# Where the activation combinations of the up-projection's first pass are computed: GpSimd or VectorE

## The chip, the core and the metric

The kernel runs on one core of a Trainium2 chip. A core has five engines that each work through a queue of their own, in order: TensorE (PE in the profile; its weight loads are PEld), VectorE (DVE), ScalarE (ACT), GpSimd (POOL) and SyncE (SP), which here only issues transfers. The engines wait for each other through semaphores. Transfers run on DMA queues; SP issues nearly all of them, in order, and a transfer that has to wait holds those behind it. The metric is the time of one execution on the device in microseconds, as a median of several runs.

## The reference

One layer of a hybrid decoder block on 2048 tokens of width 1024, all in float32: an RMSNorm, an input projection into two head groups (a gated DeltaNet and a retention group), an output projection with a residual, then the part that matters here:

```python
n2 = _rms_norm(h, mlp_norm_w[l])
h = h + _conv_glu_mlp(n2, w_up[l], mlp_conv_w[l], w_down[l])

def _conv_glu_mlp(x, w_up, conv_w, w_down):
    hdn = jnp.einsum('bsd,df->bsf', x, w_up)
    hdn = _causal_dwconv(hdn, conv_w)
    g, u = jnp.split(hdn, 2, axis=-1)
    return jnp.einsum('bsf,fd->bsd', jax.nn.silu(g) * u, w_down)
```

The up-projection has 2 × 2816 columns, the convolution is causal, depthwise, of width 3. A final RMSNorm follows.

## The kernel before

The program has three stages: the mixers, with the output projection and the second norm (about the first 1200 us), the up-projection (to about 1850 us), and the down-projection. Tokens go in four blocks of 512.

**Products.** Two ideas shape the matrix products. First, each float32 operand is split into a high half (a copy in a shorter format, made by ScalarE) and a low half (the original less the high one, made by VectorE); a product is three matmuls, high by high (line 118), high by low (119) and low by high (120). Where TensorE waits for a low half, the row shows VectorE as the releaser. Second, the products are done on 2 × 2 blocks with seven products in place of eight. For that both sides need sums and differences of blocks. `comb` makes them: in `prep_x` for the activations (line 1121), in `load_w` for the weights (line 1151). Their split is in `split` (ScalarE line 1101, VectorE line 1102).

**The up-projection.** It runs in two passes q over the tokens, each of 1024 tokens (two blocks), and in each pass over 22 groups g of columns. `prep_x(q)` loads the normed activations of the pass from DRAM (`xr`, line 1113), in four k-tiles of four blocks b11, b12, b21, b22; each tile gives four combinations, two of them chained:

```python
t1 = comb(5, ALU.subtract, b12, b11)
t2 = comb(6, ALU.subtract, b22, t1)
t3 = comb(7, ALU.subtract, b22, b12)
t4 = comb(4, ALU.subtract, b21, t2)
```

and then seven operands are split, b11, b21, b22 and the four combinations. So a pass has 16 combinations of 128 × 512 and 28 splits. They stay in SBUF for the whole pass. `xr` has seven buffers, and `st`, which holds combinations of activations and of weights, has four. The weights of a group come as two loads (`wur`, line 1144). The products of a group are in `group`; its sums on VectorE are line 1183, and the convolution is line 1225.

**The handover.** The last block's output projection is still under way when the up-projection's first pass starts: its operands are split in lines 1045 and 1046, its results are added to `Cw` in line 1017 (which frees the accumulator in PSUM), with `x` from `wx` (line 1022), and stored to `hd` (1027). A fence holds back the first loads of the pass until certain transfers of the output projection have been issued. From about 1173 to 1223 us of the span all this is mixed: output projection, `prep_x(0)`, the weights of the first groups, the first products.

**What sets the order.** Every engine's queue is put together at build time by a list scheduler of the framework, which goes by its own estimate of each instruction's duration on its engine. So an instruction that is given to another engine also changes the order of its neighbours, on all engines. The second pass's `prep_x(1)` (about 1616 to 1652 us) runs the same lines.

Of the kernel before, what the change touches and what calls it, by code (L numbers as in the profile page):

```python
# [73 lines left out]
def unit(pool, tag, shape, dt=F32, **kw):  # L74

    n = int(np.prod(shape[1:]))
    t = pool.tile([P, U1], dt, tag=tag, name=tag, **kw)[:, :n]
    if len(shape) == 3:
        t = t.rearrange("p (a b) -> p a b", a=shape[1])
    elif len(shape) == 4:  # L80
        t = t.rearrange("p (a b c) -> p a b c", a=shape[1], b=shape[2])
    return t
# [1009 lines left out]
def mlp_up(ctx, tc, marks, drp, mm3, mcw, mhalo, n2d, wud, aud, w_u):  # L1092
    nc = tc.nc
    PE, ACT, DVE, POOL = nc.tensor, nc.scalar, nc.vector, nc.gpsimd
# [5 lines left out]
    def split(dst, src, lo_eng=DVE):  # L1100
        ACT.activation(dst[:, 0], src, AF.Copy)
        lo_eng.tensor_tensor(dst[:, 1], src, dst[:, 0].bitcast(F32), op=ALU.subtract)  # L1102

    def prep_x(q, fence=None):
        xc = {}
        for kt in range(4):
            qs = []
            for i in range(2):
                xr = unit(up, "xr", [P, 2, TB], bufs=NXR)
                k = 4 * i + kt  # L1110
                for t in range(2):
                    with tc.issue_after(fence[kt]) if fence else nullcontext():
                        nc.sync.dma_start(xr[:, t], n2d[2 * q + t, k // 2][k % 2])
                qs += [xr[:, 0], xr[:, 1]]
            b11, b12, b21, b22 = qs

            sts = [unit(up, "st", [P, 2, TB], bufs=NST) for j in range(2)]

            def comb(i, op, a, b_):
                t = sts[i // 6][:, (i - 4) % 2]  # L1120
                (POOL if q == 0 else DVE).tensor_tensor(t, a, b_, op=op)  # L1121
                return t
            t1 = comb(5, ALU.subtract, b12, b11)
            t2 = comb(6, ALU.subtract, b22, t1)
            t3 = comb(7, ALU.subtract, b22, b12)
            t4 = comb(4, ALU.subtract, b21, t2)
            for i, src in ((1, b11), (2, b21), (5, t1), (6, t2), (7, t3), (4, t4), (3, b22)):
                x_ = xc[i, kt] = unit(xp, f"x{i}_{kt}", [P, 2, TB], F32R, bufs=1)
                split(x_, src)
        return xc  # L1130
# [340 lines left out]
```

## Time and profile before

| | |
|---|---|
| median of 3 runs | 2479.42 us (2477.21 to 2479.72) |
| the profiled execution | 2480.82 us, its span 2479.0 us |
| TensorE busy | 2415.2 us (97%) |
| VectorE busy | 1653.4 us (67%) |
| ScalarE busy | 1008.5 us (41%) |
| GpSimd busy | 570.4 us (23%) |
| mean granted TensorE clock | 0.992 |

A row of a group tells the line, the engine and the operation, the written and the read tiles, and a count. Rows of a timeline give start and length in us; a row with "x3" is three instructions in a row, and its length goes from the first's start to the last's end. VectorE's records overlap a little: an instruction of 0.68 us is followed by the next start after 0.60 us, so starts are what is to be compared. Behind `<-` in brackets stands how long the engine had stood idle, and what ended it. "busy" of TensorE says that a matmul was in flight, not that it ran at its best pace; the count per time tells that.

### The profile page before, as it was taken

What the parts mean: (1) busy time and instruction counts of PE and PEld (TensorE: products, weight loads), DVE (VectorE), ACT (ScalarE), POOL (GpSimd) and SP (SyncE); (2) the same over time, 40 slices, a digit from 0 to 9 for tenths busy, and PEclk for the clock granted to TensorE, in tenths of its full rate; (3) what the DMA queues carried; (4) which work ended last, traced back from release to release, by engine and by line L of the source; (5) the groups of instructions that cost most, each with busy time, mean ns of one, the idle gap of its engine ahead of it and who ended that gap; (6) DMA issues with size and microseconds to landing.
All of it is one profiled execution on the core that took longest, in us unless ns stands there. A gap on an engine that the chain in (4) does not pass through costs nothing. (4 is left out here: it accounts for less than half of the span.)

```text
span 2479.0 us, 35810 instructions
## 1 busy us (share of the span) xinstructions
PE 2415.2 (97%) x12508; PEld 2024.7 (82%) x12508; DVE 1653.4 (67%) x3244; ACT 1008.5 (41%) x2125; POOL 570.4 (23%) x881
## 2 busy tenths in 40 slices
PE   9989899999999999998899999999999999999998
PEld 7877788888878888787688888878888888888887
DVE  5876865454654646436989889896575567555783
ACT  5655634344522544234554343442232224333341
POOL 1385214700183114521400110100000001422030
PEclk9999999999999999999899999999999999999999
DMA  5887866674565565647587788776646869764782
GB/s 214 292 293 276 310 223 233 238 254 163 199 227 192 188 242 177 220 149 257 192 323 289 290 307 299 293 296 251 228 147 242 282 241 292 260 209 144 234 258 97
DMA packets 281572, 590.05 MB, mean 238 GB/s; under 512 B 40560, under 2 KB 120880, under 8 KB 281392
## 3 DMA queue, kind: packets, MB, share of 16 engines
q1 hardware_dynamic: 264528, 573.40, 65.6%
q10 hardware_dynamic: 16864, 14.37, 1.9%
q8 instruction: 98, 1.61, 0.3%
q14 instruction: 82, 0.67, 0.1%
HBM read 395.42 MB, written 192.25 MB: 237 GB/s over the span
## 5 line engine op out<-in xcount | busy, mean ns | idle before, releaser
L119 PE MATMUL p<-x,wu 128*128 128x512 f32 x1176 | 460.5, 392 | 6.3 <-DVE x L1102 6.3
L118 PE MATMUL p<-x,wu 128*128 128x512 f32 x1176 | 455.4, 392 | 2.4 <-DVE Cw L1017 1.8
L120 PE MATMUL p<-x,wu 128*128 128x512 f32 x1176 | 452.9, 391 | 0.9 <-DVE wu L1102 0.9
L561 PE MATMUL tok<-wc,n 128*128 128x512 f32 (+2 forms) x768 | 275.7, 362 | 6.0 <-ACT n L449 5.7
L562 PE MATMUL tok<-wc,n 128*128 128x512 f32 (+2 forms) x768 | 274.8, 359 | 0.0
L563 PE MATMUL tok<-wc,n 128*128 128x512 f32 (+2 forms) x768 | 273.8, 360 | 0.0
L119 PEld LDWEIGHTS p<-x,wu 128*128 128x128 f32 x1176 | 221.9, 189 | 55.2 <-DVE x L1102 9.7
L118 PEld LDWEIGHTS p<-x,wu 128*128 128x128 f32 x1176 | 222.2, 189 | 52.6 <-DVE uc L1183 2.7
L120 PEld LDWEIGHTS p<-x,wu 128*128 128x128 f32 x1176 | 221.9, 189 | 47.2 <-DVE wu L1102 1.4
L1225 DVE SCALAR_TENSOR_TENSOR acc<-uc,base,acc 128x1023 f32<-128x1023 f32 (+1 forms) x176 | 221.1, 1279 | 41.8 <-ACT acc L1222 41.6
L1183 DVE TENSOR_TENSOR uc<-p,uc 128x512 f32<-128x512 f32 x224 | 153.0, 686 | 109.5 <-PE p L120 109.0
L118 PE MATMUL d<-v,uu 128*128 128x512 f32 x448 | 174.3, 389 | 0.0
L119 PE MATMUL d<-v,uu 128*128 128x512 f32 x448 | 174.3, 389 | 0.0
L120 PE MATMUL d<-v,uu 128*128 128x512 f32 x448 | 174.3, 389 | 0.0
L220 POOL TENSOR_TENSOR vt<-vr 128x512 f32<-128x512 f32 x33 | 51.2, 1561 | 514.9 <-DVE u L1307 421.2
L561 PEld LDWEIGHTS tok<-wc,n 128*128 128x128 f32 x768 | 145.4, 190 | 25.6 <-ACT n L449 5.7
L563 PEld LDWEIGHTS tok<-wc,n 128*128 128x128 f32 x768 | 145.3, 189 | 19.9
L562 PEld LDWEIGHTS tok<-wc,n 128*128 128x128 f32 x768 | 145.4, 189 | 19.2
L119 PE MATMUL chm<-n,wc 128*128 128x512 f32 x384 | 151.7, 395 | 0.0
L118 PE MATMUL chm<-n,wc 128*128 128x512 f32 x384 | 151.6, 395 | 0.0
L120 PE MATMUL chm<-n,wc 128*128 128x512 f32 x384 | 151.6, 395 | 0.0
L771 POOL TENSOR_TENSOR pers<-Nb,pers 128x248 f32<-128x248 f32 (+30 forms) x248 | 120.1, 484 | 71.8 <-DMA Nb<-z 55.9
(258 smaller groups left out, 4843.4 us busy)
## 6 DMA issues: line engine op xcount, KB each, us to landing
wu<-wu SPq DMA_DIRECT2D x280, 512.0 KB, 6.4
wc<-wd SPq DMA_DIRECT2D x166, 512.0 KB, 5.4
wv<-wo SPq DMA_DIRECT2D x112, 512.0 KB, 6.2
wd<-wc SPq DMA_DIRECT2D x60, 512.0 KB, 4.5
ur<-au SPq DMA_DIRECT2D x56, 512.0 KB, 5.3
wur<-in_w_u SPq DMA_DIRECT2D x48, 512.0 KB, 5.6
au<-st SPq DMA_DIRECT2D x88, 256.0 KB, 4.3
vr<-in_w_d SPq DMA_DIRECT2D x77, 256.0 KB, 5.1
```

Of the source, the lines that this page charges most:

```text
L118: PE.matmul(ps, ah, bh, start=(first and i == 0), stop=False, skip_group_check=chk)
L119: PE.matmul(ps, ah, bl, start=False, stop=False, skip_group_check=chk)
L120: PE.matmul(ps, al, bh, start=False, stop=(i == n - 1), skip_group_check=chk)
L220: POOL.tensor_tensor(tt[:, j], a, b_, op=ALU.subtract)
L561: PE.matmul(ps, ah, wh, start=(k == 0), stop=False)
L562: PE.matmul(ps, ah, wl, start=False, stop=False)
L563: PE.matmul(ps, al_, wh, start=False, stop=(k == KT - 1))
L771: POOL.tensor_tensor(tm[:, :, :n], Nb[:, j:j + 1, j + 1:].to_broadcast([P, 8, n]), X[:, :, j:j + 1].to_broadcast([P, 8, n]), op=ALU.mult)
L1183: add = lambda o, ps, a: DVE.tensor_tensor(o, ps, a, op=ALU.add)
L1225: DVE.scalar_tensor_tensor(acc[:, t:], u[:, :T2 - t], w, acc[:, t:], op0=ALU.mult, op1=ALU.add)
```

## The change

In `prep_x` the engine of the combinations was GpSimd in the first pass and VectorE in the second; now it is VectorE in both. Formulas, order in the source, fences, buffers and the loads are as they were.

```diff
             def comb(i, op, a, b_):
                 t = sts[i // 6][:, (i - 4) % 2]
-                (POOL if q == 0 else DVE).tensor_tensor(t, a, b_, op=op)
+                DVE.tensor_tensor(t, a, b_, op=op)
                 return t
```

Since the scheduler puts the queues together anew, neighbours move as well. The first place is VectorE's queue at the start of the handover. `st` written from `xr` (line 1121) is a combination of activations, `st` from `wur` one of weights; `wu` with a number is an operand of the output projection, `wu` without one a weight of the first group.

```order
 L1151 TENSOR_TENSOR st<-st,wur 128x512
+L1121 TENSOR_TENSOR st<-xr 128x512
 L1017 TENSOR_TENSOR Cw<-wo,Cw 128x512
 L1151 TENSOR_TENSOR st<-wur,st 128x512
 L1046 TENSOR_TENSOR wu_12009<-co,wu_12009 128x512
-L1102 TENSOR_TENSOR wu<-st,wu 128x512 x3
+L1102 TENSOR_TENSOR wu<-st,wu 128x512 x2
+L1121 TENSOR_TENSOR st<-xr,st 128x512
+L1121 TENSOR_TENSOR st<-xr 128x512
+L1102 TENSOR_TENSOR wu<-st,wu 128x512
```

The combinations of the first k-tile now stand between the splits of the first group's weights, and the rest are spread over the next 50 places.

The second place is VectorE's queue at the end of the handover, up to the split of the last combination of the last k-tile, `x_3_12254`; the number behind `x_` is the k-tile. Before:

```order
L1102 TENSOR_TENSOR x_3_12245<-st,x_3_12245 128x512
L1151 TENSOR_TENSOR st<-wur 128x512
L1102 TENSOR_TENSOR x_3_12257<-xr,x_3_12257 128x512
L1017 TENSOR_TENSOR Cw<-wo,Cw 128x512
L1102 TENSOR_TENSOR x_2_12221<-st,x_2_12221 128x512
L1151 TENSOR_TENSOR st<-st,wur 128x512
L1102 TENSOR_TENSOR x_3_12248<-st,x_3_12248 128x512
L1151 TENSOR_TENSOR st<-wur 128x512
L1102 TENSOR_TENSOR x_3_12251<-st,x_3_12251 128x512
L1151 TENSOR_TENSOR st<-wur,st 128x512
L1102 TENSOR_TENSOR x_3_12254<-st,x_3_12254 128x512
```

And the same end in the changed kernel:

```order
L1102 TENSOR_TENSOR x_3_12245<-st,x_3_12245 128x512
L1017 TENSOR_TENSOR Cw<-wo,Cw 128x512
L1151 TENSOR_TENSOR st<-wur 128x512
L1102 TENSOR_TENSOR x_2_12221<-st,x_2_12221 128x512
L1017 TENSOR_TENSOR Cw<-Cw,wx 128x512
L1121 TENSOR_TENSOR st<-xr,st 128x512
L1102 TENSOR_TENSOR x_3_12251<-st,x_3_12251 128x512
L1102 TENSOR_TENSOR x_3_12248<-st,x_3_12248 128x512
L1151 TENSOR_TENSOR st<-st,wur 128x512
L1151 TENSOR_TENSOR st<-wur 128x512
L1017 TENSOR_TENSOR Cw<-wo,Cw 128x512
L1102 TENSOR_TENSOR x_3_12254<-st,x_3_12254 128x512
```

Two additions of the output projection have moved in front of the last split, and the last weight combination behind it.

The third place is SP's queue, where the loads of the next group's weights stand between loads of activations (`xr`; those numbered 71 to 74 are already for the second pass), loads of `x` (`wx`) and stores of the output projection's result (`hd`). Before:

```order
L1113 DMA xr<-n2d_1_72 128x512
L1144 DMA wur<-in_w_u 128x1024
L1022 DMA wx<-in_x 128x512
L1144 DMA wur<-in_w_u 128x1024
L1027 DMA hd_82<-Cw 128x1024
L1022 DMA wx<-in_x 128x512
```

Now:

```order
L1022 DMA wx<-in_x 128x512
L1113 DMA xr<-n2d_1_72 128x512
L1022 DMA wx<-in_x 128x512
L1027 DMA hd_82<-Cw 128x1024
L1144 DMA wur<-in_w_u 128x1024 x2
```

Both loads of the weights now stand behind the last load of `x` and one more store.

## The prediction

> **What bounds the kernel now.** I read the page first (busy shares, the 40 slices), then the waits of TensorE from the up-projection on, and then the place that the change touches, in windows and instruction by instruction.
>
> ```profile
> span 2479.0 us, 35810 instructions
> PE 2415.2 (97%) x12508; PEld 2024.7 (82%) x12508; DVE 1653.4 (67%) x3244; ACT 1008.5 (41%) x2125; POOL 570.4 (23%) x881
> ```
>
> TensorE is the bound of the whole. So GpSimd's share is worth nothing by itself; a change to it pays only where TensorE stands still. The windows show such a place (columns: stretch, its length, busy time and count of each engine, the granted TensorE clock, DMA share, GB/s):
>
> ```profile
> core 0: us, PE busy (x) PEld busy (x) DVE busy (x) ACT busy (x) POOL busy (x), PEclk, DMA share, GB/s
> 1173.30:1222.70 49.40, 35.95 (x114) 24.82 (x113) 49.40 (x55) 21.95 (x39) 30.12 (x17) 0.83 0.58 202
> 1222.70:1272.10 49.40, 49.40 (x235) 41.09 (x234) 41.38 (x61) 30.01 (x47) 3.72 (x9) 1.00 0.76 272
> 1400.00:1500.00 100.00, 100.00 (x441) 82.24 (x440) 88.56 (x122) 40.96 (x62) 11.65 (x11) 1.00 0.78 289
> ```
>
> At its steady pace TensorE starts 441 matmuls in 100 us, one per 0.227 us. In the 49.4 us of the handover it starts 114, worth 25.9 us: 23.5 us are lost. In the same stretch VectorE is busy 49.40 of 49.40 us, with only 55 instructions, though the next 49.4 us hold 61 in 41.4 us. So VectorE is full here, and its instructions are long. TensorE's waits in this neighbourhood (us in total, times, longest) name it:
>
> ```profile
> PE p L119 <- DVE x L1102: 6.3, 5, 3.7
> PE wo L120 <- DVE wu L1046: 3.0, 3, 2.4
> PE p L118 <- DVE Cw L1017: 1.8, 1, 1.8
> PE p L120 <- DVE wu L1102: 0.9, 1, 0.9
> ```
>
> These are the low halves of the split inputs, of the output projection's operands and of the weights, and the additions that free an accumulator. Behind 1223 us the whole list of TensorE's waits is two rows:
>
> ```profile
> PE p L1190 <- ACT x L1101: 1.8, 1, 1.8
> PE p L118 <- DVE uc L1183: 0.5, 1, 0.5
> ```
>
> So what TensorE gains in the handover it keeps: nothing later is waiting for a transfer whose time is fixed.
>
> Why are the instructions long? All that VectorE does here is 512 columns wide. Two rows of its timeline with GpSimd idle, two with GpSimd at work (start, length of the row, count at the end):
>
> ```profile
> 1185.12 1.88 DVE L1102 TENSOR_TENSOR wu<-st,wu 128x512 fp32r<-128x512 f32 x3
> 1186.92 0.68 DVE L1102 TENSOR_TENSOR wu<-wur,wu 128x512 fp32r<-128x512 f32 x1
> 1195.75 5.12 DVE L1102 TENSOR_TENSOR x<-xr,x 128x512 fp32r<-128x512 f32 x3
> 1200.79 1.76 DVE L1102 TENSOR_TENSOR x<-st,x 128x512 fp32r<-128x512 f32 x1
> ```
>
> Three starts take 1186.92 − 1185.12 = 1.80 us, 0.60 each; and 1200.79 − 1195.75 = 5.04 us, 1.68 each. The second kind lies under these rows of GpSimd:
>
> ```profile
> 1195.22 1.75 POOL L1121 TENSOR_TENSOR st<-xr 128x512 f32<-128x512 f32 x1
> 1196.94 1.71 POOL L1121 TENSOR_TENSOR st<-xr,st 128x512 f32<-128x512 f32 x1
> 1198.61 3.39 POOL L1121 TENSOR_TENSOR st<-xr 128x512 f32<-128x512 f32 x2
> ```
>
> The combinations come one per 1.7 us, in step with the long VectorE instructions. Going down VectorE's timeline from 1173.5 to 1222.9 us I count 16 starts that are some 1.7 us apart, and GpSimd has 16 combinations there. The window agrees: 54 full instructions at 0.60 and one of 0.06 would be 32.5 us of the 49.4, an excess of 16.9 us, 1.06 for each combination; by the starts it is 1.68 − 0.60 = 1.08.
>
> **The change, part by part.** *Removed:* 16 combinations from GpSimd, and with them 16 × 1.08 = 17.3 us of standing still on VectorE (16.9 by the window). *Added:* 16 combinations on VectorE. Their price needs no guess, since the second pass runs the same line there already:
>
> ```profile
> L1121 POOL TENSOR_TENSOR st<-xr x8: 1657/1734/4224, 1173.5 to 1213.5; 128x512 f32<-128x512 f32 x8
> L1121 POOL TENSOR_TENSOR st<-xr,st x8: 1370/1712/1741, 1176.0 to 1215.2; 128x512 f32<-128x512 f32 x8
> L1121 DVE TENSOR_TENSOR st<-xr x8: 686/687/689, 1616.6 to 1648.4; 128x512 f32<-128x512 f32 x8
> L1121 DVE TENSOR_TENSOR st<-xr,st x8: 684/686/689, 1621.4 to 1652.0; 128x512 f32<-128x512 f32 x8
> ```
>
> 687 ns is the length of the other short ones (0.68), so the pitch is 0.60 too: 16 × 0.60 = 9.6 us. VectorE is full, so nothing hides them, and nothing hides what goes. Net on VectorE: 17.3 − 9.6 = **7.7 us less**.
>
> [...]
>
> *Checked at the end of the stretch.* The last split that the first groups need is this one; the stretch's first long instruction stands at the other end:
>
> ```profile
> 1174.14 2.35 DVE L1046 TENSOR_TENSOR wu<-co,wu 128x512 fp32r<-128x512 f32 x2
> 1222.24 0.68 DVE L1102 TENSOR_TENSOR x<-st,x 128x512 fp32r<-128x512 f32 x1
> ```
>
> In the old order the second stands 52 starts behind the first, in the new one 69: the 16, two additions of the output projection that now stand in front of it, and one weight combination that now stands behind. 68 × 0.60 + 0.06 (one start is a tiny one) = 40.9 us, so 1215.0 in place of 1222.24: 7.2 earlier, and 7.8 for equal work.
>
> *Moved.* (a) The combinations now queue in order on VectorE, so a load that is not in holds all behind it: splits for TensorE, additions that free accumulators. The loads of the inputs:
>
> ```profile
> 1177.19 5.56 SPq L1113 DMA_DIRECT2D xr<-n2d  x8
> DMA to landing us min/median/max: 2.5/5.9/7.8
> ```
>
> The first tile's lie in front of these (GpSimd used them at 1173.5). The eight are issued by 1182.75, and with the longest landing in by 1190.6; VectorE reaches the second tile's first combination 27 starts behind 1174.14, at 1190.3. Cost 0 to 0.3 us; I take 0. (b) A combination goes to ScalarE (copy, 0.62) and back to VectorE. Between a combination and its split other work stands nearly everywhere; where too little does, VectorE pauses about 0.7 us. Three such places are the most I find: 0 to 2.1 us; I take 0, as this row of the second pass, laid out the same way, shows VectorE full too (44.00 of 44.00), with TensorE losing little (184 matmuls are 41.8 us):
>
> ```profile
> 1616.00:1660.00 44.00, 42.09 (x184) 33.98 (x183) 44.00 (x66) 22.87 (x35) 2.56 (x3) 1.00 0.79 296
> ```
>
> (c) On SP's queue the weights of the next group now stand behind two small loads and two stores; these wait for VectorE's additions, which are themselves 6 to 8 us earlier:
>
> ```profile
> 1222.95 0.33 SPq L1144 DMA_DIRECT2D wur<-in_w_u  x1
> 1218.03 0.68 DVE L1017 TENSOR_TENSOR Cw<-wo,Cw 128x512 f32<-128x512 f32 x1
> ```
>
> So the weights too should be issued before 1222.95. Cost 0; without that cover the next group starts late by one landing, some 5 us, of which the window behind (VectorE 41.38 of 49.40) would take up part. (d) TensorE's order changes with the splits; the matmuls are the same.
>
> *Sum.* The profiled execution took 2480.8 us (span 2479.0 and 1.8 around it): 2480.8 − 7.7 = 2473.1. It lies 1.4 us above the median of the runs shown, 2479.4, so for the median **2471.7 us**. With (a) and (b) at their worst the gain is 17.3 − 9.6 − 2.4 = 5.3; at best TensorE also saves the 1.8 us in front of Cw and part of its spells at half clock, a gain of up to 10.5. The likeliest case's own range is 2469 to 2474.4.
>
> **Rivals.** *The clock eats it (no change).* After a long wait TensorE runs at about half clock:
>
> ```profile
> 1200.92 0.50 PE L119 MATMUL p<-x,wu 128*128 128x512 f32 x1 [3.66 <-DVE x L1102]
> 1203.00:1213.00 10.00, 9.12 (x21) 5.72 (x21) 10.00 (x12) 4.23 (x7) 5.08 (x4) 0.53 0.19 52
> ```
>
> Behind a wait of 3.66 us, 21 matmuls in 10 us at a granted 0.53. Today that spell lies where VectorE is late anyway. If one falls instead on the end of the handover, where TensorE works off what is ready, 21 matmuls at 0.43 for 0.23 cost up to 4.2 us; with two pauses of (b) the gain is 7.7 − 4.2 − 1.4 = 2.1: 2477.3 us, within 0.2%. For it: TensorE still has only 25.9 us of work in the shorter stretch of about 41.7, 62%. Against: the single waits become shorter. Chance 0.15. [...]
>
> *VectorE pays and gets nothing (slower).* If the long instructions had another cause, such as the inputs' transfers that run at the same time, the 17.3 us stay and the 9.6 are added: 2479.4 + 9.6 = 2489 us. It decides if fewer than 9 of the 16 shorten (9.6 / 1.08). For it: the inputs land up to 1190.6, beside the first of the long ones. Against: 16 and 16; and the long ones between 1203 and 1213 have DMA at 0.19 beside them (row above). That GpSimd does not lose the work is no rival: the new order has no combination on it. Chance 0.07.
>
> *More than the sum (faster).* Accumulators are freed earlier, the splits come in an order that matches what TensorE runs next, and the half-clock spells go: gain 11 to 13, some 2467.5 us. The 23.5 us lost leave room; VectorE at 40.9 us against 25.9 of matmuls does not. Chance 0.08.
>
> **How the numbers follow.** About 0.2% (5 us, 2474.5 and 2484.4) is what a measurement of this kernel can tell from no change. Forecast 0.70, no change 0.15, slower 0.07, more 0.08: faster 0.78, same 0.15, slower 0.07. The range for 8 in 10 takes the likeliest case whole and half of both neighbours: 2467.7 to 2477.
>
> **What would show it.** In the new profile: no line L1121 on GpSimd and 32 of about 687 ns on VectorE; no VectorE split near 1.7 us between 1173 and 1215; GpSimd's busy time near 570.4 − 29.5 = 541; VectorE's total about 8 lower, though it has 16 instructions more; the last split and TensorE's full pace about 8 us earlier, and the span with them. Wrong would be: long splits without GpSimd; VectorE idle in front of L1121 for a load or for ScalarE; a granted clock near 0.5 in the last 10 us of the handover; or a new wait of TensorE behind it that gives the gain back.

## The result

The changed kernel takes 2472.73 us (median of 9 runs, 2470.93 to 2477.53), the kernel before beside it 2477.36 us (median of 9, 2474.95 to 2480.77). The ratio is 0.9978, with a 95% interval from 0.9969 to 0.9987: faster by 3.2 to 7.7 us, 4.6 by the medians. Forecast were 2471.7 us and a gain of 7.7. The time came out within 1.0 us, and that is partly luck: the kernel before measured 2 us lower beside it than in the runs shown at first (2479.42). The gain is the harder test, and it fell some 3 us short. The rest of this document is about those 3 us.

**The profile after.** First the page's totals:

```profile
span 2469.1 us, 35787 instructions
PE 2408.9 (98%) x12508; PEld 2022.4 (82%) x12508; DVE 1642.7 (67%) x3260; ACT 1010.1 (41%) x2125; POOL 549.2 (22%) x865
```

VectorE has 16 instructions more and 10.7 us less busy time. GpSimd has 16 fewer, but its busy time fell by only 21.2 us, not by the 29.5 that the combinations had taken. The groups of line 1121 show that nothing of it is left on GpSimd:

```profile
L1121 DVE TENSOR_TENSOR st<-xr x16: 683/694/702, 1178.0 to 1638.5; 128x512 f32<-128x512 f32 x16
L1121 DVE TENSOR_TENSOR st<-xr,st x16: 682/694/701, 1181.6 to 1642.1; 128x512 f32<-128x512 f32 x16
```

The same stretches as before the change, in windows (columns as in the prediction):

```profile
1173.30:1222.70 49.40, 37.65 (x135) 25.54 (x136) 45.44 (x77) 26.54 (x48) 15.99 (x1) 0.93 0.60 218
1193.00:1203.00 10.00, 7.09 (x25) 4.38 (x25) 10.00 (x18) 5.10 (x10) 10.00 (x1) 1.00 0.19 57
1203.00:1213.00 10.00, 4.97 (x12) 3.60 (x13) 6.04 (x11) 4.10 (x7) 3.27 (x1) 0.66 0.24 79
1213.00:1223.00 10.00, 9.68 (x41) 6.96 (x40) 10.00 (x18) 5.69 (x12) 0.00 (x0) 1.00 0.58 199
```

TensorE starts 135 matmuls in the handover where it started 114, and VectorE 77 instructions where it started 55. Two things were not forecast: VectorE is no longer full (45.44 of 49.40 us; the missing 3.96 all lie between 1203 and 1213), and GpSimd, which has one instruction there, is busy for 15.99 us with it. Between 1203 and 1213 TensorE starts only 12 matmuls. The timelines of the three engines show how these hang together. GpSimd and VectorE (start, length, and in brackets the idle time ahead and what ended it):

```profile
1190.29 15.99 POOL L1031 TENSOR_TENSOR pers<-pers,base 128x1 f32<-128x1 f32 x1 [47.12 <-DVE pers L1030]
1190.05 0.16 DVE L1030 TENSOR_SCALAR pers<-pers 128x1 f32<-128x1 f32 x1
1190.11 0.69 DVE L1102 TENSOR_TENSOR x<-st,x 128x512 fp32r<-128x512 f32 x1
...
1205.16 0.70 DVE L1121 TENSOR_TENSOR st<-xr,st 128x512 f32<-128x512 f32 x1
1208.01 0.69 DVE L1102 TENSOR_TENSOR x<-st,x 128x512 fp32r<-128x512 f32 x1 [2.15 <-ACT x L1101]
...
1211.71 0.69 DVE L1102 TENSOR_TENSOR x<-st,x 128x512 fp32r<-128x512 f32 x1 [1.81 <-ACT x L1101]
```

ScalarE and TensorE in the same stretch:

```profile
1206.31 1.15 ACT L1032 ACTIVATE Cw<-Cw,pers 128x1024 f32<-128x1024 f32 x1 [6.52 <-POOL pers L1031]
1207.36 0.61 ACT L1101 ACTIVATE x<-st 128x512 fp32r<-128x512 f32 x1
1210.57 0.60 ACT L1205 ACTIVATE uc<-p 128x512 f32<-128x512 f32 x1 [2.59 <-PE p L120]
1208.03 0.80 PE L118 MATMUL p<-x,wu 128*128 128x512 f32 x1 [5.50 <-ACT x L1101]
```

Line 1031 is the power (x to the −½) of the second norm, an instruction of 128 × 1 on GpSimd; this is the first of the last block's four, and it took 1.00 us in the kernel before. Here it lasts from 1190.29 to 1206.28. VectorE starts 26 two-input instructions without a break from 1190.11 to 1205.16, the last ends at 1205.86, and 0.42 us after that the power is done. ScalarE waits 6.52 us for it in front of line 1032, and because its queue is in order, the copy that a split needs (1207.36) waits behind. So TensorE stands for 5.50 us and VectorE for 2.15; TensorE's late matmul then delays ScalarE at 1210.57, and VectorE stands another 1.81 us. 2.15 + 1.81 = 3.96.

**A yardstick.** The executions differ by some us before the handover begins. So stages are counted below from T0, the start of the four additions of the output projection that every version has (in the two kernels):

```profile
1171.14 2.48 DVE L1017 TENSOR_TENSOR Cw<-wo,Cw 128x512 f32<-128x512 f32 x4 [2.87 <-PE wo L120]
```

```profile
1170.20 2.48 DVE L1017 TENSOR_TENSOR Cw<-wo,Cw 128x512 f32<-128x512 f32 x4 [2.87 <-PE wo L120]
```

The windows of the 80 us from T0, the kernel before and then the changed one, say what the handover is worth:

```profile
1171.14:1251.14 80.00, 66.55 (x256) 50.08 (x255) 76.11 (x96) 41.66 (x70) 32.76 (x23) 0.89 0.62 221
```

```profile
1170.20:1250.20 80.00, 67.60 (x283) 50.15 (x282) 70.02 (x115) 47.76 (x80) 20.57 (x8) 0.96 0.68 247
```

256 matmuls against 283: 27 × 0.227 = 6.1 us between these two executions. The whole stretch from T0 to the end of the span is a second measure, which leaves out what varies before T0: 2479.0 − 1171.14 = 1307.9 us before and 2469.1 − 1170.20 = 1298.9 after.

### The profile page after: what moved, and what is told of

It is laid out like the page before. It is cut to its first block, busy times and chain, and to the rows that moved or that the text cites. A ratio compares the mean times of both kernels' runs of the same rounds, so it can differ in the third digit from the quotient of the medians.

```text
span 2469.1 us, 35787 instructions
## 1 busy us (share of the span) xinstructions
PE 2408.9 (98%) x12508; PEld 2022.4 (82%) x12508; DVE 1642.7 (67%) x3260; ACT 1010.1 (41%) x2125; POOL 549.2 (22%) x865
## 4 chain that ended last, share of the span: by engine, by line
PE 81%; POOL 8%; DVE 4%; DMA 3%; issue 2%; ACT 1%; SPq 0%; ACTq 0%; POOLq 0%; DVEq 0%
PE p L118 11%; PE p L120 11%; PE p L119 11%; PE d L120 6%; PE d L119 6%; PE d L118 6%; PE tok L561 4%; PE tok L563 4%; PE tok L562 4%; POOL pers L773 3%; POOL pers L771 3%; PE chm L118 2%; PE chm L119 2%; PE chm L120 2%; PE wo L120 1%
## 5 line engine op out<-in xcount | busy, mean ns | idle before, releaser
L1225 DVE SCALAR_TENSOR_TENSOR acc<-uc,base,acc 128x1022 f32<-128x1022 f32 (+1 forms) x176 | 221.0, 1279 | 39.0 <-ACT acc L1222 38.9
```

Source lines behind the costliest of these rows:

```text
L1225: DVE.scalar_tensor_tensor(acc[:, t:], u[:, :T2 - t], w, acc[:, t:], op0=ALU.mult, op1=ALU.add)
```

## The experiments

Two theories went in. A: the price on VectorE is as forecast, and what is missing was eaten by the clock and by chance; the 16 us of GpSimd are a reading of one execution. B: the power is held up by VectorE's unbroken stream of two-input instructions, and ScalarE's queue carries that to the splits. Every edit also lets the scheduler put neighbours in another order.

**The changed kernel again.** No edit.

> The changed kernel once more, beside the three kernels that are compared with it. Both theories: about 4.6 us below the kernel before, as its medians had it (2472.7 against 2477.4). Theory A (the clock and chance ate the missing 3 us): the GpSimd power of 16 us, L1031 near 1190, is a reading of one execution and need not come back. Theory B (that power is held up by VectorE's unbroken stream of two-input instructions, and ScalarE's queue waits for it): it comes back with over 10 us, with a wait of ScalarE of about 6.5 us behind it and two idle times of VectorE that make about 4 us between 1205 and 1213.

2472.51 us (11 runs) against 2476.75 (21 runs of the kernel before); ratio 0.9984, interval 0.9975 to 0.9993. The power lasts 15.99 us again (from 1190.21), ScalarE waits 6.52 for it, VectorE 2.15 and 1.81, and from T0 to the end it is again 1298.9 us. The chain belongs to the kernel, not to one execution. The gain of 4.2 agrees with the first measurement.

**The power off GpSimd.** This leaves out the root in the last block: the scale there is 1/x.

```diff
-            POOL.tensor_tensor(ss[:, 8 + t:9 + t], ss[:, t:t + 1], mhalf[:, :1], op=ALU.pow)
+            DVE.reciprocal(ss[:, 8 + t:9 + t], ss[:, t:t + 1]) if b == NB - 1 else POOL.tensor_tensor(...)
```

> The changed kernel, with the power of the last block's second norm (L1031, four instructions of 128x1) left out and a reciprocal on VectorE in its place: the scale of the last block is then 1/x and not 1/sqrt(x). GpSimd has nothing left to do in the handover. Theory B: no wait of ScalarE in front of L1032 near 1199 to 1206, VectorE's two idle times of 2.15 and 1.81 us gone, the last split of the first pass at 1218.34 - 3.96 + 0.06 = 1214.4 (what was predicted for the change: 1215.0), and 4 us less than the changed kernel: about 2468.7. Theory A: the waits of ScalarE were not what set the end; within 1 us of the changed kernel, last split not before 1217.5.

2468.2 us (5 runs), ratio 0.9966 (0.9954 to 0.9979): B's 2468.7, not A's 2472.7. The windows of the stretch with the former pause, and of the 80 us from T0:

```profile
1203.00:1213.00 10.00, 8.67 (x35) 5.75 (x33) 10.00 (x18) 3.54 (x6) 0.00 (x0) 1.00 0.51 148
1251.31:1421.31 170.00, 170.00 (x752) 140.77 (x751) 153.07 (x208) 72.02 (x107) 16.73 (x18) 1.00 0.84 311
1171.31:1251.31 80.00, 70.50 (x302) 52.00 (x301) 75.22 (x124) 49.88 (x81) 1.53 (x4) 1.00 0.72 258
```

VectorE is full (10.00), TensorE starts 35 matmuls in place of 12, and the granted clock is 1.00 in all of the 80 us, where the changed kernel had 0.66 in this stretch. 302 matmuls are 19 more than the changed kernel's 283, worth 4.3 us, and the next 170 us run at the same pace in both (752). The last split of the pass stands at 1215.96, 44.65 us behind T0; in the changed kernel it was 1218.34 − 1170.20 = 48.14, in the kernel before 1222.24 − 1171.14 = 51.10.

**Making VectorE stop for the power.** Nothing is left out here: VectorE copies the power's result, and ScalarE uses the copy.

```diff
-            ACT.activation(c, c, AF.Copy, scale=ss[:, 8 + t:9 + t])
+            r = 8 + t + 4 * (b == NB - 1)
+            r > 11 and DVE.tensor_scalar(ss[:, r:r + 1], ss[:, r - 4:r - 3], 1.0, 0.0, op0=ALU.mult, op1=ALU.add)
+            ACT.activation(c, c, AF.Copy, scale=ss[:, r:r + 1])
```

> The changed kernel, with one instruction of 128x1 on VectorE behind the power, which copies its result (last block only) for ScalarE to use: VectorE must stop for it, and nothing is left out. It stands seven two-input instructions behind the tiny one that feeds the power. Theory B: the power takes about 8 x 0.60 = 5 us in place of 16, since GpSimd gets in when VectorE stops; that stop costs 0.5 to 1.0 us (in the trace the power ended 0.42 us after VectorE stood still); the idle times of 2.15 and 1.81 are gone, so 3.0 to 3.5 us less than the changed kernel: about 2469.5. Theory A: the stop is an added cost and nothing else: 0.5 to 1.0 us more, about 2473.5; the power, if it is long by itself, stays near 16 us and VectorE waits for it.

2469.67 us (5 runs), ratio 0.9967 (0.9955 to 0.998). B had said 2469.5, A 2473.5. GpSimd's power, VectorE's stop, ScalarE's line 1032, the 80 us from T0, and the stretch in which the clock is low:

```profile
1192.67 3.94 POOL L1031 TENSOR_TENSOR pers<-pers,base 128x1 f32<-128x1 f32 x1 [48.60 <-DVE pers L1030]
```

```profile
1196.65 0.15 DVE L1032 TENSOR_SCALAR pers<-pers 128x1 f32<-128x1 f32 x1 [0.45 <-POOL pers L1031]
```

```profile
1202.97 1.14 ACT L1032 ACTIVATE Cw<-Cw,pers 128x1024 f32<-128x1024 f32 x1
```

```profile
1172.58:1252.58 80.00, 71.66 (x299) 53.05 (x298) 73.55 (x123) 49.90 (x81) 10.74 (x8) 0.96 0.72 265
1193.00:1203.00 10.00, 7.84 (x18) 4.33 (x19) 9.55 (x18) 7.45 (x15) 3.62 (x1) 0.69 0.28 88
```

VectorE stops once, for 0.45 us, and the power is through. It ends 0.41 us after VectorE stands still (1196.61 against 1196.20), as it did in the changed kernel (0.42); so the length of 16 us was not its own. ScalarE's wait is gone, 299 matmuls start (16 more, 3.6 us), and the last split stands at 1217.20 − 1172.58 = 44.62 behind T0. The clock is low here too, 0.69 between 1193 and 1203, though TensorE has no wait above 1.3 us in the handover; the gain came all the same, so the clock is not what had eaten it. Nor is the order: the queues of all engines are those of the changed kernel up to about 1224 us, but for the one copy.

**The same once more,** for its interval.

> The version with the copy of the power's result on VectorE once more, for its interval: about 2469.7 and 0.3% below the kernel before, with the power at 3.9 us.

2469.95 us (5 runs) against 2477.49 (18 runs), ratio 0.9969 (0.9957 to 0.998), the power at 3.94 us in the same place. From T0 to the end it is 1295.4 us in both executions (2468.0 − 1172.58 and 2468.0 − 1172.59), 3.5 less than in those of the changed kernel. This is the version to use: 7.1 and 7.5 us below the kernel before by the medians of the two comparisons, and 2.8 below the changed one that ran beside it (2472.51).

**How GpSimd gets in.** A tiny one-input instruction of VectorE behind each combination of the first pass, for which nobody waits (`gap` is a spare tile of 128 × 1):

```diff
                 DVE.tensor_tensor(t, a, b_, op=op)
+                q == 0 and DVE.tensor_scalar(gap, t[:, :1], 1.0, 0.0, op0=ALU.mult, op1=ALU.add)
```

> The changed kernel, with a one-input instruction of 128x1 on VectorE behind each of the first pass's 16 combinations, which nobody waits for and which waits for nothing but the combination ahead of it: 16 x 0.06 = 1.0 us more on VectorE. It tells how GpSimd gets in. If any VectorE instruction that is not of the two-input kind lets it in (the tiny L1030 at 1191.74 in the kernel before: the long splits begin right behind it), the power near 1190 takes no more than the way to the next such instruction, 6 x 0.60 = 3.6 us and the power's own 0.5 to 1.0, so under 5 us in place of 16; ScalarE's wait of 6.5 us and VectorE's two idle times go, and the time is 4.0 - 1.0 = 3.0 us below the changed kernel: about 2469.6. If VectorE must stand idle for it, the power stays near 16 us and the time is 1 us above the changed kernel: 2473.6.

The mechanism came out, the time did not: 2476.09 us (12 runs), ratio 0.9995 (0.9984 to 1.0005). GpSimd's power and VectorE's next tiny instruction:

```profile
1196.53 3.95 POOL L1031 TENSOR_TENSOR pers<-pers,base 128x1 f32<-128x1 f32 x1 [48.82 <-DVE pers L1030]
```

```profile
1199.99 0.14 DVE L1121 TENSOR_SCALAR gap<-st 128x1 f32<-128x1 f32 x1
1200.05 0.67 DVE L1102 TENSOR_TENSOR x<-xr,x 128x512 fp32r<-128x512 f32 x1
```

The power ends at 1200.48, 0.49 us behind the start of the tiny instruction, with VectorE never idle there. So a tiny one-input instruction let GpSimd in; whether by its one input or by its size, this run does not tell. The windows of the 80 us from T0 (which is 1176.27 in this execution) and of the 170 behind, and TensorE's waits in the latter, tell where the gain went:

```profile
1176.27:1256.27 80.00, 71.23 (x293) 52.35 (x292) 69.17 (x128) 46.79 (x78) 9.84 (x8) 0.96 0.71 250
1256.27:1426.27 170.00, 167.27 (x733) 136.87 (x732) 151.97 (x207) 71.58 (x108) 18.38 (x17) 1.00 0.79 297
```

```profile
PE p L118 <- DVE uc L1183: 2.7, 3, 1.4
```

293 matmuls are 10 more than the changed kernel's, 2.3 us; but then 733 stand against 752, 19 fewer, 4.3 us, with TensorE waiting for VectorE's sums of groups in three places, where the changed kernel has no wait. Between 1616 and 1660, where the second pass begins, another 16 are lost (179 against 195, 3.6 us). From T0 to the end this execution takes 1304.3 us, 5.4 more than the changed kernel. The 16 extra instructions moved the order of the first groups too, which may be why; but the execution is the longest of its twelve (2482.37 us), and its handover begins 2 to 6 us later than in the other versions, so how much of this every execution loses is not shown.

**Half of the change.** Combinations 4 and 7 of the first pass stay on GpSimd, 5 and 6 go to VectorE.

```diff
-                DVE.tensor_tensor(t, a, b_, op=op)
+                (POOL if q == 0 and i in (4, 7) else DVE).tensor_tensor(t, a, b_, op=op)
```

> Half of the change: of the first pass's four combinations of each tile, two (5 and 6) on VectorE and two (4 and 7) on GpSimd. By the prediction's prices each combination that stays on GpSimd costs VectorE 1.08 us and saves it 0.60, so half of 7.7 us net: about 3.9 us below the kernel before by the sum, some 8 long VectorE instructions of about 1.7 us in the handover, last split near 1218.6. Theory B adds: GpSimd's combinations come in only where VectorE has a gap, so some of them last over 3 us, and the power L1031 stands behind them; if such a one is waited for, the gain is smaller than 3.9.

2478.42 us (11 runs), ratio 1.0003 (0.9994 to 1.0012): none of the 3.9. GpSimd and ScalarE:

```profile
1184.29 6.41 POOL L1121 TENSOR_TENSOR st<-xr,st 128x512 f32<-128x512 f32 x1 [7.30 <-PE wo L120]
1203.87 7.67 POOL L1121 TENSOR_TENSOR st<-xr,st 128x512 f32<-128x512 f32 x1 [4.24 <-DVE st L1121]
```

```profile
1190.73 0.63 ACT L1101 ACTIVATE x<-st 128x512 fp32r<-128x512 f32 x1 [5.43 <-POOL st L1121]
1211.57 1.15 ACT L1101 ACTIVATE x<-st 128x512 fp32r<-128x512 f32 x2 [7.00 <-POOL st L1121]
```

Two of the combinations that remain on GpSimd last 6.41 and 7.67 us. They end at 1190.70 and 1211.54, each 1.12 us after VectorE's stream beside them (1189.58 and 1210.42). ScalarE waits for them, 12.4 us in two, and TensorE gets no further than before: 251 matmuls in the 80 us from T0, where the kernel before had 256. VectorE's own price is not what decides here: where GpSimd did not get in, a result that was still made there was late by the length of VectorE's stream, 6.41 and 7.67 us where most combinations of the kernel before took 1.6 to 1.8. So the price per combination (1.08) holds in the mix of the kernel before and can't be scaled by their number.

**The second pass the other way.** Its combinations go from VectorE to GpSimd.

```diff
-                DVE.tensor_tensor(t, a, b_, op=op)
+                (POOL if q == 1 else DVE).tensor_tensor(t, a, b_, op=op)
```

> The changed kernel, with the combinations of the second pass moved the other way, from VectorE to GpSimd (16 of 128x512, near 1606 to 1650), where TensorE has no wait and VectorE is full (44.00 of 44.00). The prediction's price: VectorE is 16 x (1.08 - 0.60) = 7.7 us later there, of which TensorE feels between 0 and 7.7; long splits near 1.7 us. Theory B: VectorE's stream has few gaps there, so GpSimd's combinations last well over 3 us each until VectorE stands still or has another kind of instruction, and ScalarE and VectorE wait for them in turn; time 0 to 10 us above the changed kernel, 2473 to 2483. Were each combination 1.4 to 1.75 us, as most were in the kernel before, theory B would not hold there.

2485.65 us (5 runs), ratio 1.0036 (1.0023 to 1.0049): 13 us above the changed kernel, more than both bounds. GpSimd and the window:

```profile
1609.44 1.74 POOL L1121 TENSOR_TENSOR st<-xr,st 128x512 f32<-128x512 f32 x1
1631.54 5.25 POOL L1121 TENSOR_TENSOR st<-xr 128x512 f32<-128x512 f32 x1 [4.76 <-DVE x L1102]
```

```profile
1616.00:1660.00 44.00, 36.60 (x139) 27.78 (x138) 43.36 (x49) 18.03 (x27) 19.95 (x13) 0.88 0.60 216
```

Most combinations last 1.3 to 1.75 us here, so B's "well over 3 us each" is a miss: it happened to one, at 5.25. Many of VectorE's splits are long again, and 139 matmuls start in the 44 us, where the changed kernel has 195: 56 × 0.227 = 12.7 us. The contention alone, 7.7 by the prediction's price, is too small for it: TensorE also waits, 2.9 us for a sum of VectorE and 1.7 us for a split of weights among others, and its clock is 0.88 there. How the rest divides is not shown.

**The kernel before, a second profile.** No edit.

> The kernel before, looked at once more, for what its first profile had and all profiles of changed kernels lack: a TensorE wait of 1.8 us in the second pass near 1640 (184 matmuls between 1616 and 1660, where the changed kernel has 195 at the same place of the program). The code and order of the second pass are the same in both. If that wait belongs to one execution, it is gone here, the span is about 2 us shorter than 2479.0, and it is no part of the gain; if it belongs to the kernel, 184 matmuls are seen again.

The wait of 1.8 us in the second pass is gone, its window has more matmuls than the 184 of the first profile, and the span is 4.7 us shorter (2474.3):

```profile
1616.00:1660.00 44.00, 43.74 (x189) 35.00 (x188) 44.00 (x65) 19.66 (x29) 2.56 (x3) 1.00 0.79 299
1172.86:1252.86 80.00, 68.13 (x269) 50.70 (x268) 74.77 (x96) 45.12 (x73) 36.27 (x24) 0.91 0.66 230
```

So the 1.8 us belong to one execution. But 189 matmuls are still six fewer than the changed kernel's 195 at the same place, 1.4 us, and the kernel before with the stop (the next run) has 191 there. So about 1 us of the gain lies in the second pass, and what costs the kernel before that time is not shown. The handover itself varies too: 269 matmuls from T0 where the first profile had 256. Measured from this one, the change is worth 283 − 269 = 14 matmuls, 3.2 us; from the other 6.1. From T0 to the end it is worth 2.5 us (1301.4 − 1298.9) and 9.0. The 4.2 to 4.6 of the medians lie between.

**A control: the stop in the kernel before.** The edit of "Making VectorE stop", on the kernel before.

> A control: the kernel before, with the same copy of the power's result on VectorE that gave the changed kernel 3 us. There GpSimd still has the 16 combinations, the power lasts 1.00 us and ScalarE's L1032 comes only at 1211.52, so there is no wait to take away. Theory B (the change made the power late): no gain; VectorE stops for the power once, for 0 to 3 us, as GpSimd has a combination in front of it: 2477 to 2480. If the copy helps in itself (another order, or a power that was late in the kernel before too): about 3 us less than before here as well, 2474.5.

2479.47 us (12 runs) against 2479.09 (17 runs), ratio 1.0006 (0.9997 to 1.0015). No gain. GpSimd's rows say why there is nothing to take away:

```profile
1186.91 5.08 POOL L1121 TENSOR_TENSOR st<-xr 128x512 f32<-128x512 f32 x1 [6.84 <-PE wo L120]
1191.95 1.00 POOL L1031 TENSOR_TENSOR pers<-pers,base 128x1 f32<-128x1 f32 x1
```

There the combination in front is the one that is held up (5.08 us), and the power goes through behind it in 1.00. From T0 to the end it is 1303.3 us, between the two executions of the kernel before. The late power is a product of the change.

**A probe at another place.** Four GpSimd additions of 128 × 1 in the second pass of the changed kernel, which nobody waits for, written to a spare tile `gap`.

```diff
                 DVE.tensor_tensor(t, a, b_, op=op)
+                q == 1 and i == 4 and POOL.tensor_tensor(gap, t[:, :1], t[:, 1:2], op=ALU.add)
```

> The changed kernel, with four GpSimd additions of 128x1 in the second pass (one behind the last combination of each tile), which nobody waits for: the same question at another place and with another operation. Theory B: an instruction that takes under 1.1 us by itself lasts as long as VectorE's unbroken run of two-input instructions on SBUF, which near 1616 to 1625 are up to 16 in a row (9 us): at least two of the four last over 2 us, and each ends within 1.1 us behind a gap, a tiny one-input instruction or one with an operand in PSUM (L1183) on VectorE. If the power was long for a reason of its own, all four last under 1.1 us. The time stays within 1 us of the changed kernel in the stretch up to there.

They last 3.44, 0.20, 1.11 and 1.24 us: one over 2 us where two were expected. GpSimd's first three, and what VectorE ran as each came through:

```profile
1620.36 3.44 POOL L1121 TENSOR_TENSOR gap<-st 128x1 f32<-128x1 f32 x1 [1.38 <-DMA wu<-wu]
1629.90 0.20 POOL L1121 TENSOR_TENSOR gap<-st 128x1 f32<-128x1 f32 x1 [6.09 <-DVE st L1121]
1640.11 1.11 POOL L1121 TENSOR_TENSOR gap<-st 128x1 f32<-128x1 f32 x1 [10.01 <-DVE st L1121]
```

```profile
1623.66 2.48 DVE L1225 SCALAR_TENSOR_TENSOR acc<-uc,base,acc 128x1023 f32<-128x1023 f32 x2
1629.67 0.69 DVE L1183 TENSOR_TENSOR uc<-p,uc 128x512 f32<-128x512 f32 x1
1641.08 1.29 DVE L1183 TENSOR_TENSOR uc<-p,uc 128x512 f32<-128x512 f32 x2
```

The first ends at 1623.80, 0.14 us into the first instruction of another kind, and the third at 1641.22, as far into one that reads one operand from PSUM. The second falls beside such an instruction as a whole, and takes 0.20 us, the shortest of the four. So the hold-up is not special to the power. That only one of the four lasted over 2 us fits lines 1183 and 1225, which break VectorE's stream there (1623.66, 1629.67 and 1641.08 above).

## Why the prediction was right and where it was not

- **What bounds it:** right. The handover was VectorE's, with starts 1.68 us apart beside GpSimd's combinations. With these gone, starts are 0.60 us apart throughout the handover, but for VectorE's two pauses, and no split near 1.7 us is left.
- **The net of 7.7 us:** right in size, as far as medians tell, but the change alone did not collect it. The changed kernel alone gained 4.2 to 4.6. With the late power taken away the gain is 7.1 to 7.5 (VectorE stops once) and 8.6 (2476.75 − 2468.2, power left out). The last split is 6.5 us earlier from T0 in both of these; 7.2 was forecast, and the changed kernel had 51.10 − 48.14 = 3.0. About 1 us of each gain lies in the second pass, where the prediction had none.
- **(a) the loads:** right, VectorE never stands in front of line 1121 for one.
- **(b) pauses for ScalarE, taken as 0 with a bound of 2.1: this is the step that failed.** They came to 3.96 us. The reason is not the round trip that the step had in mind: with the power left out VectorE is full in the handover (49.40 of 49.40 us between 1173.30 and 1222.70). ScalarE stood 6.52 us for the power, and the copy behind it was late. The step looked only at ScalarE's copies and not at what stands among them in ScalarE's queue, line 1032, and at the engine that feeds it. The row of the second pass that served as model has three short GpSimd instructions (2.56 us), and ScalarE waits for none of them in it. The edit emptied GpSimd's queue but for this one instruction of 128 × 1, and I took a queue with less work to be a faster one.
- **(c) the weights' loads:** right, issued from 1220.73 in place of 1222.95. One more store stands in front of them, not two as the step says.
- **Busy times:** GpSimd forecast 541, found 549.2: the power's waiting adds 15 us, and the copies of line 1230 take 6.8 us less (39.8 before, 33.0 now). VectorE forecast about 8 lower, found 10.7.
- **The clock:** a spell at 0.66 came, between 1203 and 1213 and not in the last 10 us; without the power there is none. With VectorE's stop there is one as well (0.69), behind waits of at most 1.3 us where the prediction had seen one behind 3.66, and the gain came nevertheless. What starts and ends a spell is not shown by these runs. As a rival of its own it fell; whether the spells cost a little is not shown.
- **VectorE pays and gets nothing:** fell. **More than the sum:** the gain of 11 to 13 did not come, even without the power.
- **Behind the handover:** no new wait, as forecast. Of the old one in the second pass, quoted as part of the list, the 1.8 us were of one execution.
- **The sums** come out, but for the upper end of the likeliest case: a gain of 5.3 gives 2479.4 − 5.3 = 2474.1, not 2474.4.

## What to carry to other kernels

When work is taken off GpSimd and put on a VectorE that is already full, look at every instruction that stays on GpSimd there, however small, and at the queue of whoever waits for it: it may now last as long as VectorE's stream (15.99 us here in place of 1.00). Where such a result is needed, let VectorE stop once for it (0.45 us here, for 2.8 us gained) or take it off GpSimd too. A move by halves can be worth nothing (2478.42 us here beside 2476.75).

## What the hardware showed that was not expected

An instruction of 1.00 us on GpSimd lasted 15.99 us beside 26 two-input instructions of VectorE in a row, and 3.94 and 3.95 us where the stream was broken after six. An addition that took 0.20 us elsewhere lasted 3.44. What let them in was a VectorE that stood still (the power ended 0.41 and 0.42 us later), a one-input instruction of 0.14 us, or the start of an instruction of line 1183 or 1225 (0.14 us into it).

Some of the combinations that come to a running stream after GpSimd stood idle are held up in the same way (4.22 us in the kernel before, 5.08 with the stop in it, 6.41 and 7.67 in the half). Others are not: in the kernel before the one at 1204.91 takes 1.66 us after 1.23 us of idleness, and the one at 1211.94 takes 1.62 us there and 4.03 in the second profile. Those queued directly behind another mostly take turns with VectorE, one each per 1.7 us. What decides between a turn and a hold-up is not shown by these runs.

That a two-input instruction came to its end was not enough to let the power in: the 26 of the row of 15.99 us start 0.60 us apart, and the power ended only behind the last. Why the tiny instruction and those of lines 1183 and 1225 let GpSimd in, and these did not, is not shown by these runs.
